# Entry into the up-projections of a two-layer trunk: the closing norms and the first unit as a written table of named pieces

## The chip, the cores and the metric

The kernel runs on one core of one Trainium2 chip, in float32. The metric is the device time of one execution in microseconds (us), the median of several runs. Engines: PE is the matrix engine (TensorE, PEld its weight loads), DVE is VectorE, ACT is ScalarE, POOL is GpSimd, SP issues transfers.

## What is computed

Two layers on a sequence of 1024 tokens with 1024 features. Layer 0 mixes tokens by differential attention, layer 1 by multi-head latent attention (MLA). Each is followed by a gated MLP with a causal convolution of width 3 behind its up-projection.

```python
D_MODEL = 1024; SEQ = 1024; DEPTH = 2; FFN_HIDDEN = 2816
def rms_norm(x, g):
    xf = x.astype(jnp.float32)
    y = xf * lax.rsqrt(jnp.mean(xf * xf, axis=-1, keepdims=True) + NORM_EPS)
    return (y * g.astype(jnp.float32)).astype(x.dtype)
def conv_ffn(h, w_up, conv_w, conv_b, w_down):
    u = h @ w_up
    c = lax.conv_general_dilated(
        u, conv_w[:, None, :].astype(u.dtype), window_strides=(1,),
        padding=[(CONV_WIDTH - 1, 0)], dimension_numbers=('NWC', 'WIO', 'NWC'),
        feature_group_count=u.shape[-1]) + conv_b
    g, val = jnp.split(c, 2, axis=-1)
    return (jax.nn.silu(g) * val) @ w_down
def reference(...):
    ...
    for i in range(DEPTH):
        h = rms_norm(x, attn_norm_g[i])
        ...
        x = x + attention(h, ...) @ w_o   # differential in layer 0, latent in layer 1
        h = rms_norm(x, ffn_norm_g[i])
        x = x + conv_ffn(h, ffn_w_up[i], ffn_conv_w[i], ffn_conv_b[i], ffn_w_down[i])
    return rms_norm(x, final_norm_g)
```

## The kernel before

**Products.** Each float32 operand is split into a high part in a reduced format (`high`, a cast on ACT) and a low part, the rest (`low`, a subtraction on DVE, or on POOL where `gp` is passed). `mm3` makes a product of three matmuls (lines 119 to 121). The up-projection is cut into 22 units. A unit is one gate block and one value block of 128 hidden features each, and is made of seven products instead of eight, by sums of blocks: the weights' side has A11, A12, A22 and the sums S1 to S4, the tokens' side B11, B21, B22 and the sums T1 to T4. B11, B21 come from token tiles 0 to 3 and B12, B22 from 4 to 7, each transposed by PE; index q numbers the four tiles of a half. `ORDER0` pairs them and gives the order of the products in unit 0.

**The end of the output projection.** `project_rest` takes the eight token tiles in pairs 0, 4, 1, 5, 2, 6, 3, 7. For each: the second half of the output projection, the residual add, mean square on ACT (`squares`), its power −1/2 on POOL (`root`, line 167), the norm on DVE (line 958), the transposes (`turn`, line 855), sums on DVE (`sub`, line 886) and splits. The last tile, 7, is normed in two halves of 512 columns (add at line 890, mean at 966, norm at 977). Layer 1 splits T2 and the first tile of B22 early (argument `early`); layer 0 does not, and splits T2.0 and T2.1 behind the last norm, with the lows on POOL (lines 979 to 981).

**Unit 0.** The generator `up` prepares weights: `sum_of` makes S1 to S4 (line 1042), `high` and `low` split them, `prepare(upto)` does so up to a number with the low on POOL. The seven products of unit 0 are issued as fourteen halves of 256 columns in the order of `FIRST`, 12 matmuls each. Behind each half come the adds that join the products into gate and value (lines 1131 to 1138), the next entry of `late` (transposes, sums and splits of the last tiles) and `prepare` up to the next entry of `ahead`. From unit 1 on a product is 512 columns wide, and its splits are made three and four products ahead.

**What sets the order.** From `project_rest` to the end of the up-projection PE and DVE run in the order in which the code issues (`outer`), POOL in the entry as well (`inner`). ACT's order in the entry is chosen by the scheduler, which also orders the attentions by itself. Transfers run on SP's queue; a weight block is fetched once its buffer is free.

Of the kernel before, what the change touches and what calls it, by code (L numbers as in the profile page):

```python
# [13 lines left out]
ALU = mybir.AluOpType  # L14
# [4 lines left out]
P = 128  # L19
# [37 lines left out]
class Trunk:  # L57
# [767 lines left out]
    def project_rest(self, W, o_d, os, X, at, x_d, g, junk, places, sums, early, begin):  # L825
# [20 lines left out]
        def normed(i, cols):  # L846
            return ends[cols.start] if i == NT - 1 else X[i][:, cols]

        def turn(i):
            names = ("B11", "B21") if i < 4 else ("B12", "B22")  # L850
            for name, cols in zip(names, (first, rest)):
                ps = banks[name, i % 4] = self.bank("u" if name == "B22" else "b")
                x = normed(i, cols)
                for k in range(4):
                    nc.tensor.transpose(ps[:, k * P : (k + 1) * P], x[:, k * P : (k + 1) * P], self.ident)
# [31 lines left out]

        def add(i, y, cols=slice(0, D)):
            x, to = X[i]
            dve.tensor_add(to[:, cols], x[:, cols], y[:, cols])  # L890

        def store(i):
            X[i] = X[i][1]
            nc.sync.dma_start(x_d[i * P : (i + 1) * P, :], X[i])

        def both(name, q, eng=dve):
            high(name, q)
            low(name, q, eng)
# [58 lines left out]
                        both("T2", q, gp)  # L957
            dve.scalar_tensor_tensor(X[before], X[before], r.pop(before), g, ALU.mult, ALU.mult)
# [7 lines left out]
        dve.tensor_scalar(s1, s1, 1.0 / D, EPS, ALU.mult, ALU.add)  # L966
        add(7, y, rest)
        s2 = self.squares(X[7][1][:, rest], junk[:, rest])
        store(7)
        start.sum("S1")  # L970
        sub("T4", 2)
        high("B11", 3)
        r7 = self.root(s2, D, s1)
        start.part(2, dve)
        for cols, place in ((first, "h12"), (rest, "h13")):
            ends[cols.start] = self.at(place, [P, 512])
            dve.scalar_tensor_tensor(ends[cols.start], X[7][:, cols], r7, g[:, cols], ALU.mult, ALU.mult)
        high("B21", 3)
        if "T2" not in early:
            both("T2", 0, gp)  # L980
            both("T2", 1, gp)
        low("B11", 3)
        low("B21", 3)

        def steps(*todo, now=lambda: None):
            def then():
                for f, *args in todo:
                    f(*args)

            return now, then  # L990

        late = [
            steps(),
            steps(),
            steps((copy, 3), (high, "B22", 3), (sub, "T1", 3), (both, "T1", 3, gp), (sub, "T3", 3), (low, "B22", 3), now=lambda: turn(7)),
            steps((sub, "T2", 3), (sub, "T4", 3)),
            steps((both, "T3", 0), (both, "T4", 0)),
            steps(*(() if "T2" in early else ((both, "T2", 2),)), (both, "T3", 1)),
            steps((both, "T2", 3), (both, "T4", 1)),
            steps((both, "T3", 2), (both, "T3", 3)),  # L1000
            steps((both, "T4", 2)),
            steps((both, "T4", 3)),
        ]
# [5 lines left out]
    ORDER0 = [("A11", "B11"), ("A12", "B21"), ("S1", "T1"), ("S4", "B22"), ("S2", "T2"), ("S3", "T3"), ("A22", "T4")]  # L1009


    FIRST = [(j, slice(256 * half, 256 * half + 256)) for j, half in (
        (0, 0), (1, 0), (2, 0), (0, 1), (1, 1), (3, 0), (2, 1), (3, 1), (4, 0), (4, 1), (5, 0), (5, 1), (6, 0), (6, 1))]

    def up(self, layer, pl, g_d, follow):

# [11 lines left out]
        def fetch(f):  # L1028
            if f < NF:
                raws[f] = [self.fetch(a["ffn_up"][layer, half * NF + f], D) for half in range(2)]  # L1030

        def sum_of(f, name):
            (gate, val) = raws[f]
            if (f, name) not in made:
                x, y, op = {
                    "S1": lambda: (val[:, first], val[:, rest], ALU.add),
                    "S2": lambda: (sum_of(f, "S1"), gate[:, first], ALU.subtract),
                    "S3": lambda: (gate[:, first], val[:, first], ALU.subtract),
                    "S4": lambda: (gate[:, rest], sum_of(f, "S2"), ALU.subtract),
                }[name]()  # L1040
                made[f, name] = sums([P, 512])
                nc.vector.tensor_tensor(made[f, name], x, y, op)  # L1042
            return made[f, name]

        def high(upto):

            while done.hi <= upto:
                n = done.hi
                done.hi += 1
                f = n // 7  # L1050
                if f >= NF:
                    continue
                name = order(n)[0]
                gate, val = raws[f]
# [21 lines left out]
            high(n)  # L1076
            low(n, eng or nc.gpsimd)

        T, late, region, inner = yield SimpleNamespace(part=part, sum=lambda name: sum_of(0, name))

        def products(n, out, cols, onto=False):
            w, t = W[n], T[order(n)[1]]
            for k in range(4):
                wh, wl = (w[:, part, k * P : (k + 1) * P] for part in range(2))
                rh, rl = (t[part][:, k, cols] for part in range(2))
                self.mm3(out, wh, wl, rh, rl, k == 0 and not onto, k == 3, onto)
# [22 lines left out]

            return SimpleNamespace(base=base, tap=tap, silu=silu, gated=gated, store=store)  # L1110

        sum_of(0, "S4")
        high(3)

        ahead = [3, 3, 3, 3, 3, 5, 6, 7, 8, 8, 8, 9, 9, 10]
        one, two = self.big(), self.big()
        bank = dict(A11=one[:, rest], S1=one[:, first], S3=one[:, rest], A22=two[:, first], S4=two[:, rest], A12=two[:, first])
        outs = {}
        for j, cols in self.FIRST:
            name = order(j)[0]  # L1120
            out = outs.get(j, bank.get(name))
            if out is None:
                out = outs[j] = self.bank("u")
            products(j, out[:, cols], cols)
            now, then = late.pop(0) if late else (lambda: None, lambda: None)
            if cols.stop == 512:
                if name == "A11":
                    u = gate, val = [self.at(place, [P, S]) for place in pl.u[:2]]
                    nc.scalar.copy(val[:, first], out)
                elif name == "S2":  # L1130
                    add(gate[:, rest], out, val[:, first])
                elif name == "S3":
                    add(val[:, rest], out, gate[:, rest])
                    add(gate[:, rest], bank["S1"], gate[:, rest])
                elif name == "A12":
                    add(gate[:, first], out, val[:, first])  # L1136
                elif name == "A22":
                    add(val[:, first], out, val[:, rest])
                    add(val[:, rest], bank["S1"], val[:, rest])
                if j == 6:  # L1140
                    add(gate[:, rest], bank["S4"], gate[:, rest])
            now()
            if j == 1:
                low(3, nc.gpsimd)
            then()
            upto = ahead.pop(0)
            if upto == 7 and 1 not in raws:
                fetch(1)
            prepare(upto)


        inner.close()
# [1156 lines left out]
```

## Time and profile before

| what | us |
|---|---|
| three runs | 2411.99, 2414.26, 2412.88 |
| median | 2412.88 |
| the profiled execution | 2414.68 |
| its span | 2412.9 |
| its mean granted clock of PE | 0.995 |

All durations below come from the profiled execution; its own time is 1.8 above its span and 1.8 above the median of the runs. A row of a timeline gives the start from the span's begin, the length, engine, line, operation, output and inputs, shapes and count, and in brackets the idle time before it with what ended it. A row of a group ends in busy time, mean length in ns, and idle time before. Lengths of pipelined matmuls overlap: start to start counts. Buffers are named by place and number (u3, h12, s9; b, u, S and big ones are PSUM), so names tell the kind of tile and not its content.

### The profile page before, as it was taken

How to read it: one execution, taken by the hardware profiler on the slowest of the kernel's cores; microseconds unless marked ns; L12 is line 12 of the kernel's file. 1: busy time of each engine (PE TensorE's matmuls, PEld its weight loads, DVE VectorE, ACT ScalarE, POOL GpSimd, SP SyncE). 2: the span in 40 equal slices, each digit the busy share in tenths (PEclk: the TensorE clock that was granted, in tenths of full speed). 3: DMA queues.
4: the chain of work that ended last, by engine and by line, in shares of the span. 5: the costliest groups of instructions: out<-in, count | busy, mean ns of one | idle time of the engine just before them, and what ended most of it. 6: DMA issues, size and time to landing. Idle time of an engine off the chain costs nothing.

```text
span 2412.9 us, 32605 instructions
## 1 busy us (share of the span) xinstructions
PE 2353.4 (98%) x11936; PEld 2000.5 (83%) x11936; DVE 1953.6 (81%) x3175; ACT 1290.7 (53%) x2366; POOL 621.2 (26%) x489
## 2 busy tenths in 40 slices
PE   7999999999999999999999999999999999999998
PEld 7888888887888888788898789988888888887886
DVE  6888888758888888899864788886588888888997
ACT  5677767744444444444445777775354444443443
POOL 4555555324000000000132666664330000000001
PEclk9999999999999999999999999999999999999999
DMA  4111111333222222643222111123322222227502
GB/s 154 40 36 36 36 48 53 110 109 106 79 79 88 88 79 79 231 166 98 81 90 64 60 40 40 40 93 107 114 71 88 87 79 79 87 83 275 175 1 79
DMA packets 95792, 213.91 MB, mean 89 GB/s; under 512 B 8720, under 2 KB 33936, under 8 KB 95632
## 3 DMA queue, kind: packets, MB, share of 16 engines
q1 hardware_dynamic: 86448, 184.04, 23.0%
q10 hardware_dynamic: 9184, 27.79, 3.1%
q8 instruction: 94, 1.54, 0.3%
q14 instruction: 66, 0.54, 0.1%
HBM read 159.37 MB, written 52.43 MB: 88 GB/s over the span
## 4 chain that ended last, share of the span: by engine, by line
PE 85%; DVE 6%; ACT 3%; DMA 3%; POOL 1%; issue 1%; SPq 0%; POOLq 0%; DVEq 0%; ACTq 0%
PE S L119 13%; PE S L121 13%; PE S L120 13%; PE b L119 8%; PE b L120 8%; PE b L121 8%; PE u L119 4%; PE u L121 4%; PE u L120 4%; PE b L252 2%; PE u L2015 1%; DVE s L130 1%; PE u L2014 1%; PE S L1859 1%; PE S L1858 1%
## 5 line engine op out<-in xcount | busy, mean ns | idle before, releaser
L167 POOL TENSOR_TENSOR st<-st,mhalf 128x1 f32<-128x1 f32 x56 | 36.6, 655 | 1314.6 <-DVE st L164 1305.3
L119 PE MATMUL S<-s,u 128*128 128x512 f32 (+1 forms) x800 | 304.0, 380 | 6.8 <-DVE u L1136 3.7
L121 PE MATMUL S<-s,u 128*128 128x512 f32 (+1 forms) x800 | 303.0, 379 | 0.1
L120 PE MATMUL S<-s,u 128*128 128x512 f32 (+1 forms) x800 | 302.7, 378 | 0.0
L127 ACT CAST u<-h 128x512 fp32r<-128x512 f32 (+2 forms) x242 | 145.8, 619 | 279.9 <-DVE h L1042 278.9
L119 PE MATMUL b<-s,u 128*128 128x512 f32 x588 | 231.0, 393 | 1.8 <-DVE u L130 1.2
L120 PE MATMUL b<-s,u 128*128 128x512 f32 x588 | 229.3, 390 | 0.0
L121 PE MATMUL b<-s,u 128*128 128x512 f32 x588 | 229.2, 390 | 0.0
L1099 DVE SCALAR_TENSOR_TENSOR u<-u,conv,u 128x1023 f32<-128x1023 f32 (+1 forms) x176 | 225.7, 1283 | 1.4 <-ACT u L1095 1.4
L149 POOL TENSOR_TENSOR u<-u,st 128x512 f32<-128x512 f32 (+7 forms) x160 | 172.0, 1084 | 168.5 <-DVE st L2000 105.0
L127 ACT CAST s<-u 128x512 fp32r<-128x512 f32 (+3 forms) x230 | 144.7, 665 | 103.1 <-PE u L121 37.2
L119 PEld LDWEIGHTS S<-s,u 128*128 128x128 f32 x800 | 152.1, 190 | 35.6 <-ACT s L127 4.0
L130 DVE TENSOR_TENSOR u<-b,u 128x512 fp32r<-128x512 f32 (+1 forms) x256 | 158.7, 631 | 20.8 <-ACT u L127 18.2
L121 PEld LDWEIGHTS S<-s,u 128*128 128x128 f32 x800 | 152.0, 190 | 28.1 <-DVE u L130 0.5
L120 PEld LDWEIGHTS S<-s,u 128*128 128x128 f32 x800 | 152.1, 190 | 27.3
L127 ACT CAST u<-b 128x512 fp32r<-128x512 f32 (+1 forms) x256 | 134.9, 546 | 72.0 <-PE b L1905 40.5
L119 PE MATMUL u<-s,s 128*128 128x512 f32 (+1 forms) x408 | 163.4, 401 | 1.9 <-DVE s L130 0.9
L130 DVE TENSOR_TENSOR s<-u,s 128x512 fp32r<-128x512 f32 (+2 forms) x210 | 151.1, 754 | 9.7 <-ACT s L127 9.4
L121 PE MATMUL u<-s,s 128*128 128x512 f32 (+1 forms) x408 | 158.8, 389 | 0.0
L120 PE MATMUL u<-s,s 128*128 128x512 f32 (+1 forms) x408 | 158.6, 389 | 0.0
L1102 ACT ACTIVATE u<-u 128x1024 f32<-128x1024 f32 x44 | 46.7, 1062 | 187.7 <-DVE u L1099 187.6
L130 DVE TENSOR_TENSOR u<-h,u 128x512 fp32r<-128x512 f32 x164 | 112.8, 688 | 32.5 <-ACT u L127 31.5
(280 smaller groups left out, 6544.1 us busy)
## 6 DMA issues: line engine op xcount, KB each, us to landing
u<-in_ffn_up SPq DMA_DIRECT2D x88, 512.0 KB, 3.9
g_d<-u ACTq DMA_DIRECT2D x44, 512.0 KB, 2.6
u<-in_ffn_down SPq DMA_DIRECT2D x66, 256.0 KB, 5.0
u<-g_d SPq DMA_DIRECT2D x62, 256.0 KB, 4.4
s<-in_da_wqkv SPq DMA_DIRECT2D x23, 512.0 KB, 3.6
x_d<-u SPq DMA_DIRECT2D x16, 512.0 KB, 3.0
s<-x_d SPq DMA_DIRECT2D x8, 1024.0 KB, 10.8
u<-o_d SPq DMA_DIRECT2D x24, 256.0 KB, 3.0
```

What stands on the lines that cost most here:

```text
L119: mm(out, lh, rl, start=first, stop=False, skip_group_check=onto)
L120: mm(out, lh, rh, start=False, stop=False, skip_group_check=onto)
L121: mm(out, ll, rh, start=False, stop=last, skip_group_check=onto)
L127: self.nc.scalar.copy(out, src)
L130: (eng or self.nc.vector).tensor_sub(out, src, hi.bitcast(F32))
L149: self.nc.gpsimd.tensor_mul(x, x, s.to_broadcast(list(x.shape)))
L167: nc.gpsimd.tensor_tensor(r, s, self.mhalf, ALU.pow)
L252: self.nc.tensor.transpose(ps[:, j * P : (j + 1) * P], probs[t][:, k : k + P], self.ident)
L1099: nc.vector.scalar_tensor_tensor(t[half][:, back:], u[half][:, : S - back], w, t[half][:, back:], ALU.mult, ALU.add)
L1102: nc.scalar.activation(t[0], t[0], AF.Silu)
L1858: nc.tensor.matmul(sc[c][:, b : b + m], ql[c][:, qs], kt[:, c, :m], start=True, stop=False)
L1859: nc.tensor.matmul(sc[c][:, b : b + m], qh[:, c, qs], kt[:, c, :m], start=False, stop=True)
```

## The change

The closing norm of tile 7, the last transposes, sums and splits, the split of the weights of products 1 to 10, the fourteen halves of unit 0 and the adds behind them become named pieces: `x`, `ya`, `yb` are transposes (tile 3; tile 7, first and second half), `xa`, `xb` the two halves of the residual add, `xs`, `xq` their squares, `xt` the mean, `xr` the root, `ea`, `eb` the norm halves; `T1.3s`, `T1.3h`, `T1.3l`, `T1.3g` a sum, its high, its low on DVE, its low on POOL, for tile 3 of T1; `w4h`, `w4l`, `w4g` the same for the weights of product 4; `sS1`, `tS1` sums of unit 0 and of unit 1; `p3a`, `p3b` the halves of product 3; `c0` to `e6` the adds; `f1` the fetch of unit 1's weights. A table `CLOSE` lists them once for each layer, in the order in which they are issued. ACT is put under the written order in the entry as well.

```diff
-        def turn(i):
+        def turn(i, which=3):
...
-            for name, cols in zip(names, (first, rest)):
+            for name, cols in list(zip(names, (first, rest)))[which == 2 : which]:
...
-        y = ys[NT - 1]
-        turn(3)
-        X[7] = X[7], at(7, X[7])
-        add(7, y, first)
-        s1 = self.squares(X[7][1][:, first], junk[:, first])
-        start.part(1)
-        dve.tensor_scalar(s1, s1, 1.0 / D, EPS, ALU.mult, ALU.add)
-        add(7, y, rest)
...
-        if "T2" not in early:
-            both("T2", 0, gp)
-            both("T2", 1, gp)
...
-        return T, late, outer, inner
+        tokens = {}
+
+        def put(name, f, *args):
+            tokens[name] = lambda: f(*args)
+
+        put("x", turn, 3)
+        put("xa", end_add, first)
...
+        put("ya", turn, 7, 1)
+        put("yb", turn, 7, 2)
+        put("B12.3c", copy, 3)
+        for name in ("B11", "B21", "B22", "T1", "T2", "T3", "T4"):
+            for q in range(4):
+                put(f"{name}.{q}s", sub, name, q)
+                put(f"{name}.{q}h", high, name, q)
+                put(f"{name}.{q}l", low, name, q)
+                put(f"{name}.{q}g", low, name, q, gp)
+        return T, tokens, outer, inner
...
-    FIRST = [(j, slice(256 * half, 256 * half + 256)) for j, half in (
-        (0, 0), (1, 0), (2, 0), (0, 1), (1, 1), (3, 0), (2, 1), (3, 1), (4, 0), (4, 1), (5, 0), (5, 1), (6, 0), (6, 1))]
+    CLOSE = (
+        (
+            "x w1h xa w1g xs xb sS1 T4.2s B21.3h xt xq w2h T2.1h T4.0h xr T2.0h B21.3l w2l B11.3h ea eb p1a sS2 p2a sS4 w3h yb",
...
+        (
...
+            "T2.3g T1.3l p1b w6h w5l T4.3s T3.2h w6l T4.1g f1 T4.2h T4.3h p4a p5a T4.3l T3.3h p2b w7h T3.3g p4b c1 T3.2g tS1 tS3",
...
-        for j, cols in self.FIRST:
...
-                elif name == "A12":
-                    add(gate[:, first], out, val[:, first])
...
-            prepare(upto)
+            c1=lambda: add(gate_of(first), outs[1], val_of(first)),
...
+        inner.enter_context(self.tc.manual_schedule(engines={mybir.EngineType.Activation}))
+        for name in " ".join(self.CLOSE[layer]).split():
+            tokens[name]()
+        gate, val = u
```

The orders below stand at three places. First VectorE in layer 0, from the norm of tile 6 on (L958 above it): L890 the residual add of tile 7, L1042 (L1056 after) the sum S1 of the weights, L886 a sum of tokens, L130 a low, L977 (L981) the norm halves h12, h13. Before:

```order
L890 TENSOR_TENSOR u7_1061_5743<-s11_957_5148,S_1048_5672 128x512
L966 TENSOR_SCALAR st1_1062_5745<-st1_1062_5745 128x1
L890 TENSOR_TENSOR u7_1061_5743<-s11_957_5148,S_1048_5672 128x512
L1042 TENSOR_TENSOR h9_1065_5755<-u15_1052_5709 128x512
L886 TENSOR_TENSOR u6_1045_5659<-b_1042_5626,u2_1035_5600 128x512
L166 SCALAR_TENSOR_TENSOR st1_1064_5752<-st1_1064_5752,st1_1062_5745 128x1
L130 TENSOR_TENSOR u11_1067_5762<-h9_1065_5755,u11_1067_5762 128x512
L977 SCALAR_TENSOR_TENSOR h12_1068_5765<-u7_1061_5743,st1_1066_5759,u9_975_5296 128x512
L977 SCALAR_TENSOR_TENSOR h13_1069_5767<-u7_1061_5743,st1_1066_5759,u9_975_5296 128x512
L130 TENSOR_TENSOR s1_1000_5427<-b_1059_5733,s0_999_5426 128x4x128
L130 TENSOR_TENSOR s3_1003_5432<-b_1060_5738,s2_1002_5431 128x4x128
```

and in the changed kernel:

```order
L890 TENSOR_TENSOR u7_1064_5749<-s11_957_5148,S_1048_5672 128x512 x2
L1056 TENSOR_TENSOR h9_1066_5755<-u15_1052_5709 128x512
L886 TENSOR_TENSOR u6_1045_5659<-b_1042_5626,u2_1035_5600 128x512
L974 TENSOR_SCALAR st1_1065_5752<-st1_1065_5752 128x1
L166 SCALAR_TENSOR_TENSOR st1_1067_5760<-st1_1067_5760,st1_1065_5752 128x1
L130 TENSOR_TENSOR s3_1003_5432<-b_1062_5742,s2_1002_5431 128x4x128
L130 TENSOR_TENSOR u11_1068_5763<-h9_1066_5755,u11_1068_5763 128x512
L981 SCALAR_TENSOR_TENSOR h12_1074_5778<-u7_1064_5749,st1_1073_5771,u9_975_5296 128x512
L981 SCALAR_TENSOR_TENSOR h13_1075_5780<-u7_1064_5749,st1_1073_5771,u9_975_5296 128x512
L1056 TENSOR_TENSOR h10_1076_5794<-h9_1066_5755,u14_1051_5707 128x512
```

The two halves of the add stand together, the mean (L966, now L974) behind them; the low of B21.3 (s3) has moved ahead of the norm halves and that of B11.3 (s1) further back. Second GpSimd in layer 0, around the root of tile 7 (L167); s11 are lows of T2, u10 and s13 those of later weights and tokens. Before:

```order
L130 TENSOR_TENSOR u13_1063_5747<-u14_1051_5707,u13_1063_5747 128x512
L167 TENSOR_TENSOR st1_1066_5759<-st1_1064_5752,mhalf_119 128x1
L130 TENSOR_TENSOR s11_1071_5771<-u0_989_5373,s10_1070_5770 128x4x128
L130 TENSOR_TENSOR s11_1071_5771<-u1_1011_5481,s10_1070_5770 128x4x128
L130 TENSOR_TENSOR u10_1074_5782<-h11_1073_5780,u10_1074_5782 128x512
L130 TENSOR_TENSOR s13_1017_5495<-h7_1080_5836,s12_1016_5494 128x4x128
```

and in the changed kernel:

```order
L130 TENSOR_TENSOR u13_1063_5747<-u14_1051_5707,u13_1063_5747 128x512
L167 TENSOR_TENSOR st1_1073_5771<-st1_1067_5760,mhalf_119 128x1
L130 TENSOR_TENSOR u10_1078_5810<-h11_1077_5808,u10_1078_5810 128x512
L130 TENSOR_TENSOR s11_1070_5766<-u0_989_5373,s10_1069_5765 128x4x128
L130 TENSOR_TENSOR s5_1084_5845<-u4_998_5423,s4_1083_5844 128x4x128
```

The two lows of T2 no longer follow the root directly: one has gone behind the low of S4's weights, the other to VectorE. Third PE at the start of the MLA attention, which the table does not list; S are score matmuls, L252 transposes, L2014 and L2015 (L2033 and L2034 after) products of weights with values, b_2126 a projection. Before:

```order
L121 MATMUL S_2138_12634<-s12_1963_11882,s5_2015_12099 128x256
L252 MATMUL b_2114_12542<-ident_113,u8_2097_12468 128x128 x3
L119 MATMUL b_2126_12588<-s2_1819_10968,u2_2058_12294 128x512
L120 MATMUL b_2126_12588<-s2_1819_10968,u2_2058_12294 128x512
L121 MATMUL b_2126_12588<-s2_1819_10968,u3_2059_12295 128x512
```

and in the changed kernel:

```order
L121 MATMUL S_2138_12637<-s12_1963_11885,s5_2015_12102 128x256
L119 MATMUL S_2146_12679<-s8_1964_11886,s9_2048_12250 128x384
L120 MATMUL S_2146_12679<-s8_1964_11886,s9_2048_12250 128x384
L121 MATMUL S_2146_12679<-s8_1964_11886,s9_2048_12250 128x384
L252 MATMUL b_2114_12545<-ident_113,u8_2097_12471 128x128 x3
L2033 MATMUL u_2108_12517<-u0_2101_12491,s4_2010_12089 128x256
```

The score matmuls S_2146 stand ahead of the transposes, and the products u_2108 ahead of the projection b_2126, behind which both stood before. The count of matmuls is the same in both kernels; POOL has 484 instructions instead of 489 and DVE five more.

More of the change, by code (lines that the diff above doesn't have):

```diff
@@ L972, in project_rest @@
[L972 to L978, printed above, removed]
-        if "T2" not in early:
-            both("T2", 0, gp)
-            both("T2", 1, gp)
[L982 to L1003, printed above, removed]
@@ L1004, in project_rest, with end_add, end_squares, end_mean @@
-        return T, late, outer, inner
+        last, st = ys[NT - 1], SimpleNamespace()
+        def end_add(cols):
+            if cols == first:
+                X[7] = X[7], at(7, X[7])
+            add(7, last, cols)
+        def end_squares(name, cols):
+            to = X[7][1] if cols == first else X[7][1]
+            setattr(st, name, self.squares(to[:, cols], junk[:, cols]))
+            if cols == rest:
+                store(7)
+        def end_mean():
+            dve.tensor_scalar(st.s1, st.s1, 1.0 / D, EPS, ALU.mult, ALU.add)
@@ new lines, in end_root, with end_norm @@
+        def end_root():
+            st.r = self.root(st.s2, D, st.s1)
+        def end_norm(cols):
+            ends[cols.start] = self.at("h12" if cols == first else "h13", [P, 512])
+            dve.scalar_tensor_tensor(ends[cols.start], X[7][:, cols], st.r, g[:, cols], ALU.mult, ALU.mult)
+        tokens = {}
[3 more added lines that the diff above has]
+        put("xa", end_add, first)
+        put("xb", end_add, rest)
+        put("xs", end_squares, "s1", first)
@@ L1077, in part @@
             low(n, eng or nc.gpsimd)
-        T, late, region, inner = yield SimpleNamespace(part=part, sum=lambda name: sum_of(0, name))
+        T, tokens, region, inner = yield SimpleNamespace(part=part)
         def products(n, out, cols, onto=False):
@@ L1118, in up, with begin, product @@
         outs = {}
-        for j, cols in self.FIRST:
-            name = order(j)[0]
-            out = outs.get(j, bank.get(name))
+        u = []
+        gate_of = lambda cols: u[0][:, cols]
+        val_of = lambda cols: u[1][:, cols]
+        def begin():
+            u.extend(self.at(place, [P, S]) for place in pl.u[:2])
+            nc.scalar.copy(val_of(first), outs[0])
+        def product(j, cols):
+            out = outs.get(j, bank.get(order(j)[0]))
             if out is None:
                 out = outs[j] = self.bank("u")
+            outs[j] = out
@@ L1124, in up @@
             products(j, out[:, cols], cols)
[L1125 to L1134, printed above, removed]
-                elif name == "A12":
[L1136 to L1148, printed above, removed]
-            prepare(upto)
+        for j in range(7):
+            tokens[f"p{j}a"] = lambda j=j: product(j, slice(0, 256))
+            tokens[f"p{j}b"] = lambda j=j: product(j, slice(256, 512))
+        for n in range(1, 11):
+            tokens[f"w{n}h"] = lambda n=n: high(n)
+            tokens[f"w{n}l"] = lambda n=n: low(n)
+            tokens[f"w{n}g"] = lambda n=n: low(n, nc.gpsimd)
@@ new lines, in up @@
+        for name in ("S1", "S2", "S3", "S4"):
+            tokens["s" + name] = lambda name=name: sum_of(0, name)
+            tokens["t" + name] = lambda name=name: sum_of(1, name)
+        tokens.update(
+            f1=lambda: fetch(1),
+            c0=begin,
+            c1=lambda: add(gate_of(first), outs[1], val_of(first)),
+            c4=lambda: add(gate_of(rest), outs[4], val_of(first)),
+            c5=lambda: add(val_of(rest), outs[5], gate_of(rest)),
+            d5=lambda: add(gate_of(rest), bank["S1"], gate_of(rest)),
+            c6=lambda: add(val_of(first), outs[6], val_of(rest)),
+            d6=lambda: add(val_of(rest), bank["S1"], val_of(rest)),
+            e6=lambda: add(gate_of(rest), bank["S4"], gate_of(rest)),
+        )
```

15 lines of the change are left out of this document (8 added, 7 removed), and 6 rows, old and new, of the table CLOSE.

## The prediction

> **What bounds the kernel now.** I read the head of the page, then the chain that ended last, then a table of windows over the three stretches in which the order changes.
>
> ```profile
> span 2412.9 us, 32605 instructions
> PE 2353.4 (98%) x11936; PEld 2000.5 (83%) x11936; DVE 1953.6 (81%) x3175; ACT 1290.7 (53%) x2366; POOL 621.2 (26%) x489
> PE 85%; DVE 6%; ACT 3%; DMA 3%; POOL 1%; issue 1%; SPq 0%; POOLq 0%; DVEq 0%; ACTq 0%
> ```
>
> TensorE is busy 98% of the span and the number of its matmuls stays, so all that the change can win are stretches in which TensorE stands or crawls. The windows below are: the entry of layer 0, from the transposes of token tile 3 to the first matmul of unit 1; the equally long stretch behind it; the same two for layer 1; and the start of the MLA attention. Columns: start and end, length, busy time and count of PE, PEld, DVE, ACT, POOL, granted clock, DMA share, GB/s.
>
> ```profile
> 571.89:602.51 30.62, 25.49 (x184) 23.77 (x185) 28.56 (x36) 11.50 (x23) 16.22 (x11) 0.94 0.26 87
> 602.51:633.13 30.62, 30.62 (x137) 25.36 (x136) 25.31 (x33) 15.06 (x21) 2.56 (x2) 1.00 0.22 70
> 1755.06:1783.24 28.18, 24.45 (x186) 23.54 (x186) 25.47 (x35) 12.67 (x26) 15.15 (x11) 0.94 0.23 76
> 1783.24:1811.42 28.18, 28.18 (x127) 23.34 (x126) 23.40 (x30) 13.90 (x19) 2.55 (x2) 1.00 0.17 57
> 1347.00:1432.00 85.00, 84.05 (x536) 75.57 (x536) 67.51 (x162) 61.85 (x137) 56.35 (x45) 0.99 0.13 37
> ```
>
> Behind the entries PE is busy throughout; in them it loses time, and its clock is 0.94. In layer 0 VectorE is busy 28.56 of 30.62 us: it is the engine that paces that entry. An entry is 168 matmuls of 256 columns and 16 transposes. What they cost end to end is read from starts that follow each other without a wait (start, length, engine, line):
>
> ```profile
> 590.23 0.28 PE L119 MATMUL S<-s,u 128*128 128x256 f32 x1
> 590.35 0.28 PE L120 MATMUL S<-s,u 128*128 128x256 f32 x1
> 571.89 1.07 PE L855 MATMUL b<-ident,u 128*128 128x128 f32 x8 [0.82 <-DVE u L958]
> 572.71 0.36 PE L119 MATMUL S<-s,u 128*128 128x256 f32 x1
> ```
>
> A matmul takes 0.12 us from start to start, so 168 take 20.2; eight transposes take 0.82, so 16 take 1.6. That stream is 21.8 us. Layer 0 lost 30.6 − 21.8 = 8.8 us in the entry, layer 1 28.2 − 21.8 = 6.4. Where it went, first by what PE waited for (us in total, times, longest; layer 0, then layer 1):
>
> ```profile
> PE S L119 <- DVE s L130: 1.7, 2, 1.1
> PE u L855 <- DVE h L977: 1.1, 1, 1.1
> PE S L119 <- DVE u L1136: 1.1, 1, 1.1
> PE b L855 <- DVE h L977: 0.8, 1, 0.8
> PE S L119 <- DVE u L890: 0.2, 1, 0.2
> PE S L119 <- POOL s L130: 0.2, 1, 0.2
> ```
>
> ```profile
> PE S L119 <- DVE u L1136: 2.6, 1, 2.6
> PE S L119 <- DVE u L890: 1.0, 1, 1.0
> ```
>
> and then by the clock (window of 3.41 us, PE busy and count, granted clock, DMA share, GB/s):
>
> ```profile
> 577.79:581.20 3.41, 1.54 (x12) 1.00 0.00 0
> 581.20:584.61 3.41, 3.41 (x17) 0.50 0.02 5
> 1765.62:1769.03 3.41, 0.81 (x7) 1.00 0.01 2
> 1769.03:1772.44 3.41, 3.41 (x19) 0.50 0.00 0
> 1757.36:1760.77 3.41, 2.33 (x18) 1.00 0.38 154
> 2200.30:2203.71 3.41, 1.86 (x9) 1.00 1.05 386
> ```
>
> In both entries a window in which PE was busy 1.54 or 0.81 us is followed by one at half clock, which does 1.7 us of work in 3.41 and so costs 1.7. Windows with 1.86 and 2.33 busy were not followed by a drop. That is 1.7 of the loss in each entry; the rest is waits: 8.8 − 1.7 = 7.1 in layer 0 (5.1 recorded, plus some 0.16 for each of seven waits, since a record lasts 0.28 where the next starts after 0.12, plus short waits and changes of shape), 4.7 in layer 1 (3.6 recorded).
>
> The Trainium skill, TensorE: Matmul & The Clock Gate, Part 1, has the free-running window of 3413 ns and lets the clock fall only after an idle one. The rows above agree on the length, but the clock fell after windows that were 45% and 24% busy; by the page no stop here (at most 2.6 us) would have cost clock, and the sum below would be 3.4 smaller, 2410.4. The measured rows decide.
>
> **The change, part by part.**
>
> *Layer 0, the norm of the last tile.* The transposes of the last tile wait 0.8 and 1.1 for the two norm halves:
>
> ```profile
> 573.79 0.16 DVE L966 TENSOR_SCALAR st<-st 128x1 f32<-128x1 f32 x1 [1.45 <-ACT u L157]
> 573.87 0.68 DVE L890 TENSOR_TENSOR u<-s,S 128x512 f32<-128x512 f32 x1
> 575.89 1.05 POOL L167 TENSOR_TENSOR st<-st,mhalf 128x1 f32<-128x1 f32 x1 [3.02 <-DVE st L166]
> 576.92 2.96 POOL L130 TENSOR_TENSOR s<-u,s 128x512 fp32r<-128x512 f32 x2
> 576.98 3.45 DVE L977 SCALAR_TENSOR_TENSOR h<-u,st,u 128x512 f32<-128x512 f32 x2 [0.44 <-POOL st L167]
> 580.57 0.63 PE L855 MATMUL u<-ident,h 128*128 128x128 f32 x4 [1.11 <-DVE h L977]
> 1760.92 1.41 DVE L977 SCALAR_TENSOR_TENSOR h<-u,st,u 128x512 f32<-128x512 f32 x2 [0.44 <-POOL st L167]
> ```
>
> Two things are changed. The second residual add stood behind the small mean, which waited 1.45 us for ScalarE; now both adds go back to back, so the second starts at about 572.2 instead of 573.87, and the sums, squares and the power with it (1.4 us earlier: power about 574.4, norm halves from 575.5). And the two lows of T2 that GpSimd ran beside the norms are gone from there: beside them the halves took 3.45, in layer 1, where GpSimd has nothing beside, 1.41. So the halves end at about 576.9 instead of 580.43, 3.5 earlier. The transposes follow at 577.1 and 577.5, with 0.15 of wait, where before the second four stood at 580.57.
>
> What is late next is the split of the S1 weights, whose high is a ScalarE cast of 0.62:
>
> ```profile
> L127 ACT CAST u<-h 128x512 fp32r<-128x512 f32 (+2 forms) x242 | 145.8, 619 | 279.9 <-DVE h L1042 278.9
> ```
>
> I walk the new order with the rows' durations, each instruction starting when its engine and its sources are free. The sum S1 runs on VectorE behind the two adds, 572.8 to 573.5; its cast stands behind the square of the second half and is done at 574.8, which holds PE 0.6; its low on VectorE, until 575.6, holds PE another 0.6. After 577.1 no piece waits; the margins run from 0.5 (at 582.5) to 4 us. Waits left: 0.6 + 0.6 + 0.15 = 1.35, against 5.5 for the same walk of the old order (0.3, 0.6, 0.5, 1.4, 0.15, 1.1, 0.2, 0.2, 1.1). Gain in waits 4.2. In the 3.41 us of 574 to 577.4 PE would be busy over 2 us, above the 1.86 that kept the clock, so the half-clock window goes as well: 1.7. **Layer 0: −5.9**; unit 1 starts near 596.5.
>
> *VectorE as cover.* Its busy 28.56 us falls with the entry only if it has less to do, since unit 1 needs its splits. It does:
>
> ```profile
> L130 DVE TENSOR_TENSOR s<-u,s 128x512 fp32r<-128x512 f32 x9 | 10.3, 1191 | 0.0
> L130 DVE TENSOR_TENSOR s<-b,s 128x512 fp32r<-128x512 f32 x2 | 1.3, 676 | 0.0
> 586.90 1.74 POOL L130 TENSOR_TENSOR s<-h,s 128x512 fp32r<-128x512 f32 x1
> 585.67 1.27 POOL L130 TENSOR_TENSOR u<-h,u 128x512 fp32r<-128x512 f32 x1 [5.79 <-ACT u L127]
> ```
>
> A low whose source is in PSUM takes 0.68 on VectorE; the nine with both sources in SBUF average 1.19, because some ran beside GpSimd's, which grow from 1.27 to 1.74 at the same time. Nine times 0.51 is 4.6 us, and the norms above lost another 2.0 to it. In the new table layer 0 has five GpSimd subtractions fewer and three VectorE ones more in all. Three at 0.68 cost 2.0 and at least five collisions of about 0.5 to 1.1 go: 2.5 to 5.5. VectorE comes out 0.5 to 3.5 ahead, before the norms' 2.0. That cover is what the 0.5 margin hangs on; were it gone, each further collision would cost up to 1.1.
>
> *Layer 1.* The norms collide with nothing there, so less is to be had. The 2.6 us wait ends on the add of L1136 (gate of A12), which in program order stood before S4's first half and on VectorE behind a row of other operations. As `c1` it now stands behind p4b, and S4's first half (`p3a`) well ahead of it, so that this piece no longer waits for it. Walked waits: 4.2 before (1.1, 0.6, 2.5), 2.4 after (1.7 at 1757.3, where the low of the second weights stands behind the adds and one low, and 0.7 at 1767.7). Gain 1.8 in waits and 1.7 in clock is 3.5; my walk of the old order is 0.9 us later than the trace in this stretch, so I take between: **layer 1: −3.0**, bounds −1.2 (the clock falls anyway) to −3.5. One fetch is exposed: the sums of unit 1 need weights whose buffer GpSimd frees at 1772.4;
>
> ```profile
> u<-in_ffn_up SPq DMA_DIRECT2D x88, 512.0 KB, 3.9
> ```
>
> with 3.9 us to landing VectorE stands about 3 us at 1773.4 to 1776.6, and the last low that unit 0 needs keeps 0.3 us of margin. SP's two swapped issues are this fetch and its partner.
>
> *MLA start.* Its instructions are not in the table, but its order has come out differently: score matmuls and transposes have been drawn ahead of products. Before, PE lost little there:
>
> ```profile
> PE b L119 <- DVE u L130: 0.9, 2, 0.5
> ```
>
> The walk gives 1.5 us of waits before and 3.9 after; a part is made up before the stretch ends. **+1.2**, bounds +0.9 and +2.3. ScalarE's order in the entries is fixed now as well; with 11.5 and 12.7 us busy of about 30 it costs nothing beyond the 0.6 above.
>
> *Sum.* −5.9 − 3.0 + 1.2 = −7.7. The profiled execution took 2414.68, 1.8 above the runs' median of 2412.88, about one half-clock window. If it is one of the two in the entries that the median run lacks, the median falls by only 6.0, to 2406.9; if it lies elsewhere, it falls by 7.7 to 2405.2; from the profiled time the sum gives 2407.0. I take 2406.8.
>
> **The rivals.**
>
> *The clock still drops in layer 1.* The 1.7 us wait from 1757.3 lies in the window 1757.36 to 1760.77, busy 2.33 with a recorded wait of 1.0 before. With 1.5 recorded it would be busy about 1.8, between 1.54, which cost the clock, and 1.86, which did not. For: a low that is 0.2 us later than walked is enough; against: 1.8 is much nearer to 1.86. +1.7 on the sum: 2408.5. 24%.
>
> *The MLA start costs more.* Three new waits there end on ScalarE's and VectorE's exponential chain, whose durations in the new neighbourhood no row shows. At the whole 3.9 us without anything made up, and a little of clock, it is +4 instead of +1.2: 2409.6. 7%.
>
> *Slower: collisions of VectorE and GpSimd make VectorE the bound of both entries.* GpSimd still has some ten subtractions in each, and they fall where the table puts them, against VectorE lows of 1.19 mean and norm halves of up to 1.72. Each collision more than walked costs up to 1.1, once VectorE's surplus is used up (2.5 in layer 0 from above, 3 in layer 1 from its stand at the fetch). The gain is gone from (7.7 + 5.5) / 1.1 = 12 of them on. Were all ten in each entry to hit anew, 11 us each, layer 0 would be 11 − 2.5 − 5.9 = 2.6 longer, layer 1 11 − 3 − 3 = 5.0, and the MLA start 1.2: 8.8 over the runs' median, about 2422. For it: nine lows already lose 4.6 us, and who starts first is a matter of tenths. Against: the old order, with five more of GpSimd's in layer 0, still lost no more than 8.8 there. 5%. The Trainium skill, SBUF — State Buffer, section SBUF: two separate sides, calls that pair of ports an exclusive lock, held for the whole instruction by whoever starts first; by it the loser of each pair would stand for the other's full 1.3 us, 13 instead of 11 in each entry.
>
> *More is won.* Layer 1 gives its full 3.5, the MLA start takes 0.9, and all of it shows against the median: 2412.9 − 5.9 − 3.5 + 0.9 = 2404.4. For it: both are bounds from above; against: the walk of layer 1 was late by 0.9. 9%.
>
> **How the numbers follow.** My forecast with small spread has 55%. About 0.2% (4.8 us) is what a measurement of this kernel can tell from no change: faster means under 2408.05, slower over 2417.7. Forecast and large gain are 64%, and of the clock rival, whose 2408.5 lies just beyond that bound, a third lands below it: 0.72 faster. The rest of it and the MLA rival are 0.23; slower 0.05. The range holds the clock rival and most of the MLA one and reaches down to the larger gain: 2404.0 to 2410.5.
>
> **What would show it.** In the new trace: norm halves of about 0.75 us each ending near 577 in layer 0; no window at clock 0.50 in 571 to 600 or in the 30 us of layer 1's entry; unit 1 of layer 0 starting near 596.5, and of layer 1 near 1783.2 − 7.7 = 1775.5. Wrong would be: VectorE lows of 1.7 on PE's waits (collisions), a PE wait over 2.5 us in layer 1's entry, or PE idle growing by over 3 us in 1341 to 1426.

## The result, and the profile after

| | before | changed |
|---|---|---|
| median of eight runs, us | 2412.41 | 2405.53 |
| lowest to highest | 2411.36 to 2414.26 | 2402.48 to 2407.88 |
| profiled execution, us | 2414.68 | 2402.48 |

The ratio is 0.997 (0.9962 to 0.9979): 6.9 us less, where 2406.8 was forecast (6.1 under the median shown then). The profiled execution of the changed kernel is the fastest of its eight runs, so its trace shows a larger difference, 12.2 us. The windows below answer to those of before: layer 0's entry, layer 1's entry, the MLA start (there from the same pair of matmuls in both kernels; for before the row is shown first).

```profile
1341.18:1432.10 90.92, 87.94 (x551) 78.45 (x551) 71.72 (x173) 66.63 (x145) 62.17 (x48) 0.98 0.14 42
```

```profile
570.36:595.01 24.65, 23.09 (x186) 22.18 (x185) 24.23 (x36) 14.25 (x29) 11.39 (x9) 1.00 0.31 108
1748.12:1773.61 25.49, 22.92 (x186) 22.13 (x186) 21.93 (x34) 12.95 (x26) 11.85 (x10) 1.00 0.26 84
1333.29:1425.22 91.93, 87.05 (x551) 77.12 (x552) 72.25 (x175) 66.53 (x145) 62.16 (x48) 1.00 0.14 41
```

Layer 0's entry is 30.62 − 24.65 = 6.0 shorter, layer 1's 28.18 − 25.49 = 2.7, both at full clock now. The MLA start is 1.0 longer although its clock had been 0.98 and is 1.00. VectorE in layer 0 fell from 28.56 to 24.23 us busy: it still fills the entry. What PE waits for in the changed kernel's two entries (first layer 0, then layer 1), and over the whole MLA start, before and changed:

```profile
PE S L121 <- DVE u L130: 0.8, 1, 0.8
PE S L121 <- POOL u L130: 0.7, 1, 0.7
```

```profile
PE S L119 <- DVE s L130: 1.9, 2, 1.7
PE u L121 <- DVE u L130: 0.6, 1, 0.6
```

```profile
PE S L119 <- ACT u L1994: 2.8, 3, 1.4
PE b L119 <- DVE u L130: 0.9, 2, 0.5
```

```profile
PE S L119 <- ACT u L2013: 4.3, 5, 1.4
PE u L2033 <- DVE u L130: 0.7, 1, 0.7
PE b L252 <- DVE S L2011: 0.5, 1, 0.5
PE b L252 <- DVE u L130: 0.2, 1, 0.2
```

Seven waits in layer 0, 5.1 us, have become two of 1.5; in layer 1 3.6 have become 2.5; at the MLA start 3.7 have become 5.7. The next rows are the norm of tile 3 and the norm halves of tile 7, both on VectorE, and the root on GpSimd. The section on the change calls the norm at L958 that of tile 6; it is that of tile 3, which stands ahead of tile 7 in the pairs and whose transposes wait for it.

```profile
568.18 1.76 DVE L958 SCALAR_TENSOR_TENSOR u<-u,st,u 128x1024 f32<-128x1024 f32 x1
574.92 1.41 DVE L981 SCALAR_TENSOR_TENSOR h<-u,st,u 128x512 f32<-128x512 f32 x2
573.88 0.55 POOL L167 TENSOR_TENSOR st<-st,mhalf 128x1 f32<-128x1 f32 x1 [1.56 <-DVE st L166]
```

The halves take 1.41 instead of 3.45 and end at 576.3 instead of 580.4. The rest of the 12.2 lies outside: 1.5 ahead of layer 0's entry, 2.6 behind layer 1's, where this execution lacks a half-clock window that the other had at 2216, and 0.4 between layer 0's entry and the MLA start.

### The profile page after: what moved, and what is told of

It is laid out like the page before. It is cut to its first block, busy times and chain, and to the rows that moved or that the text cites. A ratio compares the mean times of both kernels' runs of the same rounds, so it can differ in the third digit from the quotient of the medians.

```text
span 2400.7 us, 32598 instructions
## 1 busy us (share of the span) xinstructions
PE 2345.5 (98%) x11936; PEld 1993.4 (83%) x11936; DVE 1947.9 (81%) x3180; ACT 1290.0 (54%) x2366; POOL 612.4 (26%) x484
## 4 chain that ended last, share of the span: by engine, by line
PE 85%; DVE 6%; DMA 3%; ACT 3%; POOL 2%; issue 2%; SPq 0%; POOLq 0%; DVEq 0%; ACTq 0%
PE S L119 13%; PE S L121 13%; PE S L120 13%; PE b L119 8%; PE b L120 8%; PE b L121 8%; PE u L119 4%; PE u L121 4%; PE u L120 4%; PE b L252 2%; PE u L2034 1%; PE u L2033 1%; PE S L1878 1%; PE S L1877 1%; DMA u<-g_d 1%
## 5 line engine op out<-in xcount | busy, mean ns | idle before, releaser
L167 POOL TENSOR_TENSOR st<-st,mhalf 128x1 f32<-128x1 f32 x56 | 36.1, 645 | 1312.7 <-DVE st L164 1304.9
L130 DVE TENSOR_TENSOR u<-b,u 128x512 fp32r<-128x512 f32 (+1 forms) x256 | 159.0, 632 | 21.6 <-ACT u L127 19.0
L130 DVE TENSOR_TENSOR s<-u,s 128x512 fp32r<-128x512 f32 (+2 forms) x204 | 139.1, 714 | 9.2 <-ACT s L127 8.9
L130 DVE TENSOR_TENSOR u<-h,u 128x512 fp32r<-128x512 f32 x171 | 117.4, 687 | 32.6 <-ACT u L127 31.5
```

The costliest lines, as they stand in the source:

```text
L130: (eng or self.nc.vector).tensor_sub(out, src, hi.bitcast(F32))
L167: nc.gpsimd.tensor_tensor(r, s, self.mhalf, ALU.pow)
```

## The experiments

Times are medians; the ratio to the kernel before, measured beside each on the same chip, has its 95% interval. The kernel before took 2412.41 beside the changed kernel, 2412.74 beside e1 to e4, 2412.61 beside e5 to e7 and 2413.18 beside e8 to e10. Because one half-clock window more or less moves a run by up to 1.7 us, the trace's stretches are given beside each time: an entry runs from the transposes of tile 3 to the first matmul of unit 1, the MLA start between the same two matmuls as above; in brackets half of the time that it spent at half clock, which is the most that this can have cost. It costs less where PE would have waited: the MLA start in its old order takes 90.12 with none (e8) and 91.63 with 3.4 (e10).

| kernel | time, us | ratio | layer 0's entry | MLA start | layer 1's entry |
|---|---|---|---|---|---|
| before | 2412.41 | | 30.62 (1.7) | 90.92 (1.7) | 28.18 (1.7) |
| changed | 2405.53 | 0.9962 to 0.9979 | 24.65 | 91.93 | 25.49 |
| e1 layer 1 only | 2409.46 | 0.9980 to 0.9997 | 29.61 (1.7) | 91.07 (1.7) | 25.40 |
| e2 ScalarE free | 2408.22 | 0.9970 to 0.9988 | 25.61 | 91.00 (1.7) | 28.33 |
| e3 lows beside norm | 2406.60 | 0.9967 to 0.9986 | 26.58 | 92.19 (1.7) | 25.66 |
| e4 mean between adds | 2403.86 | 0.9953 to 0.9978 | 24.97 | 91.11 (1.7) | 25.72 |
| e5 one low earlier | 2404.03 | 0.9946 to 0.9971 | 25.45 | 91.03 (3.0) | 25.71 |
| e6 gate add ahead | 2407.32 | 0.9965 to 0.9986 | 25.47 | 91.04 (3.2) | 29.25 (1.7) |
| e7 old order, ScalarE fixed | 2419.99 | 1.0018 to 1.0037 | 32.51 (1.7) | 91.50 (3.1) | 31.67 (1.4) |
| e8 layer 0 only | 2406.29 | 0.9960 to 0.9982 | 25.44 | 90.12 | 28.16 (1.7) |
| e9 changed, again | 2404.40 | 0.9953 to 0.9978 | 24.62 | 92.82 (3.4) | 27.42 |
| e10 as e5, again | 2404.47 | 0.9948 to 0.9975 | 25.44 | 91.63 (3.4) | 25.59 |

**e1: layer 1's table alone.** Layer 0 runs the old code.

```diff
-        up = k.up(0, pl, g_d[0], follow)
-        operands = k.project_rest(
+        up = k.up_old(0, pl, g_d[0], follow)
+        operands = k.project_rest_old(
```

> Layer 0 keeps the old order and layer 1 alone has its table; the MLA start then stands as before. Theory (the two entries gain separately, 6 us in layer 0 and 3 in layer 1): layer 1's entry about 3 us shorter, layer 0's unchanged with its two late norm halves of 1.7 us each and its half-clock window, time 3 under before, about 2409.5. Rival (layer 1 owes its gain to the window of half clock alone): the waits of layer 1's entry sum to as much as before, and its time is within 1.7 of before, 2410.7 to 2412.4.

3.3 us faster; layer 1's entry is 25.40 as in the changed kernel, layer 0's 29.61 with its late norm halves and its half-clock window, and the MLA start stands as before. The rival, that only a window of half clock had been gained, would have left layer 1's waits as they were: they fell from 3.6 to 2.4.

**e8: layer 0's table alone**, with the one low of e5 moved so that the MLA start keeps its old order; layer 1 runs the old code.

```diff
-        up = k.up(1, pl, g_d[1], follow)
-        operands = k.project_rest(
+        up = k.up_old(1, pl, g_d[1], follow)
+        operands = k.project_rest_old(
```

> Layer 0 has its table (with the one low moved, so that the MLA start stands as before) and layer 1 keeps the old order: only layer 0's entry differs from the kernel before. Theory (the parts add up): layer 0's entry 6 us shorter, layer 1's as before with its 2.5 us wait on the gate's add; 2406.0 to 2407.0, and with the 3.3 measured for layer 1 alone it makes the 8.6 of both. Rival (the two entries share a part of the gain, such as a window of half clock that only moves on): under 4.5 gained, over 2408.

6.9 us faster; layer 0's entry 25.44, layer 1's 28.16 with the old wait and its half clock:

```profile
PE S L119 <- DVE u L1132: 2.6, 1, 2.6
...
PE S L119 <- DVE u L890: 1.0, 1, 1.0
```

6.9 and 3.3 make 10.2, and both with the old MLA start gave 8.6 (e5) and 8.7 (e10). In the traces the parts add up better: 5.2 and 2.8 of entry are 8.0, where both entries together gave 7.6 (e5) and 7.8 (e10). The difference in the times is within the intervals of about 2.5 us each.

**e2: ScalarE's order free.** The tables stay.

```diff
-        inner.enter_context(self.tc.manual_schedule(engines={mybir.EngineType.Activation}))
```

> The tables stay, but ScalarE's order in the entries is left to the scheduler as before; this also gives the MLA start its old order back. Theory of the prediction (ScalarE's fixed order is worth nothing, the new order of the MLA start costs 2.3): entries as in the changed kernel, 2.3 gained at the MLA start, about 2403.2. Rival (the fixed order of ScalarE is a part of the gain, because a cast that a low and a piece of PE wait for is otherwise behind squares and casts that nobody waits for yet): layer 0's entry 2 us longer than in the changed kernel, with PE waits of 1.2 and 0.8 and two of 0.6; layer 1's up to 4 longer, with waits of 2.2, 1.7 and 1.8; with the 2.3 gained about 2409.5.

The rival holds, at somewhat less than the size it was given. In layer 0 PE waits on ScalarE's cast (first row), and layer 1 loses its whole gain, 28.33 at full clock, with the waits of the other rows:

```profile
PE S L119 <- ACT u L127: 1.0, 1, 1.0
```

```profile
PE S L119 <- DVE s L130: 2.1, 1, 2.1
PE b L855 <- DVE u L886: 1.5, 1, 1.5
...
PE S L121 <- DVE u L130: 0.6, 1, 0.6
```

ScalarE in layer 1 shows why. Casts keep it busy from 1750.52 to the square of tile 7's first half, which starts at 1753.61, although the residual add that it needs began at 1751.89 and took 0.7; in the changed kernel (last row) ScalarE is free and the square starts as soon as that add is done:

```profile
1750.52 2.71 ACT L127 CAST s<-u 128x512 fp32r<-128x512 f32 x5 [0.20 <-PE S L121]
1753.61 0.63 ACT L157 ACTIVATE u<-u 128x512 f32<-128x512 f32 x1
```

```profile
1749.10 0.63 ACT L157 ACTIVATE u<-u 128x512 f32<-128x512 f32 x1 [1.52 <-DVE u L890]
```

The MLA start has its old order. The two entries are 25.61 + 28.33 − 24.65 − 25.49 = 3.8 longer, and the stretch ahead of layer 0's entry is 1.0 longer (last section); 1.2 is given back at the MLA start, and the time is 2.7 longer. So 3.8 us of the entries' gain hang on ScalarE following the table, the engine that is busy 53% of the span in the kernel before. The rest does not: with ScalarE free the tables are still 4.5 us faster than the kernel before, and layer 0's entry keeps 5.0 of its 6.0.

**e7: that fixing alone.** The old code, with ScalarE held to its issue order.

```diff
+        inner.enter_context(self.tc.manual_schedule(engines={mybir.EngineType.Activation}))
         ahead = [3, 3, 3, 3, 3, 5, 6, 7, 8, 8, 8, 9, 9, 10]
```

> The kernel before with one part of the change alone: ScalarE held to the order in which the old code issues, in both entries. Theory (fixing ScalarE pays only with the table, since in the old code casts stand behind casts that nobody needs yet): layer 0's entry 2.5 longer than before, with PE waits of 2.5 and 3.0, layer 1's 2.1 longer with waits of 2.4 and 3.2; about 2417. Rival (the fixed order is by itself worth the 2 and 4 us that freeing it cost): about 2406 to 2408.

2419.99 against 2412.61 for the kernel before on the same chip, 7.4 slower. The direction was expected, the size was not: layer 0's entry is 1.9 longer, layer 1's 3.5 and the MLA start 0.6. The profiled executions are 4.3 apart, so the rest of the 7.4 is not placed by a trace. The longest waits in layer 0:

```profile
PE S L119 <- DVE s L130: 3.2, 2, 2.3
PE u L855 <- DVE h L977: 1.1, 1, 1.1
PE S L119 <- DVE u L1137: 1.0, 1, 1.0
```

So the fixing is worth something only with the table, in which casts stand in the order of need; the table is worth 4.5 us without the fixing (e2), 5.0 in layer 0's entry and nothing in layer 1's.

**e3: the two lows of T2 back beside the norm.**

```diff
-            "... xr T2.0h B21.3l ... yb", "T2.1l w3g ... p0b T2.0g ...",
+            "... xr T2.0h T2.0g T2.1g B21.3l ... yb", "w3g ... p0b ...",
```

> One part of the table undone in layer 0: the lows of T2.0 and T2.1 go back onto GpSimd right behind the root, beside the two norm halves. Theory (VectorE and GpSimd exclude each other there): the norm halves take about 3.4 us together instead of 1.4, VectorE is 1.5 to 2 us late behind them, and PE waits about 1.5 for the low of B22.3 (the product S4's second half); entry 1.5 longer, time about 2407.0, the MLA start as in the changed kernel. Rival (the two adds side by side made the gain, the lows are hidden by the margins): norm halves long, but no new PE wait over 0.3, time 2405.5.

VectorE first, then GpSimd, then what PE waits for:

```profile
575.40 2.44 DVE L981 SCALAR_TENSOR_TENSOR h<-u,st,u 128x512 f32<-128x512 f32 x2
577.76 1.75 DVE L1056 TENSOR_TENSOR h<-h,u 128x512 f32<-128x512 f32 x1
575.79 3.18 POOL L130 TENSOR_TENSOR s<-u,s 128x512 fp32r<-128x512 f32 x2 [0.88 <-ACT s L127]
```

```profile
PE u L855 <- DVE h L981: 1.0, 1, 1.0
PE S L121 <- DVE u L130: 0.8, 1, 0.8
PE S L121 <- POOL u L130: 0.7, 1, 0.7
PE S L119 <- DVE s L130: 0.6, 1, 0.6
```

The two GpSimd lows stretch one norm half and the sum behind it, 1.0 us each (2.44 for two against 1.41, 1.75 for one against 0.68). The entry is 1.9 longer, where 1.5 was expected, and the new waits sit on the norm half (1.0) and a low (0.6), where a wait of 1.5 on the low alone was expected.

**e4: the mean between the two adds again.**

```diff
-            "x w1h xa w1g xs xb sS1 T4.2s B21.3h xt xq ...",
+            "x w1h xa w1g xs xt xb sS1 T4.2s B21.3h xq ...",
```

> One part of the table undone in layer 0: the small mean stands between the two halves of the residual add again, where VectorE waits for ScalarE's square. This also gives the MLA start its old order back, with ScalarE's order still fixed. Theory: VectorE waits about 1 us at the mean, PE's waits on the split of the S1 weights grow by 0.4 and 0.3, layer 0's entry is 0.75 longer, and 2.3 is gained at the MLA start: about 2404.0. Rival (the new order of the MLA start costs nothing): about 2406.3.

```profile
573.00 0.15 DVE L974 TENSOR_SCALAR st<-st 128x1 f32<-128x1 f32 x1 [0.85 <-ACT u L157]
```

VectorE waits 0.85 us for the square again and the entry is 0.3 longer; 0.75 was expected. This swap of two pieces gives the MLA start its old order: 91.11, where the changed order at the same half clock (e3) has 92.19.

**e6: the gate's add ahead of S4** (on e5's table).

```diff
-            "... T3.0g w4h T4.0g sS3 p3a T4.1h ... T1.3l p1b w6h ... w7h T3.3g p4b c1 T3.2g ...",
+            "... T3.0g w4h T4.0g sS3 T4.1h ... T1.3l p1b c1 p3a w6h ... w7h T3.3g p4b T3.2g ...",
```

> As the previous kernel, and in layer 1's table the add c1 (gate of A12) goes directly behind p1b and the first half of S4 (p3a) behind it, as both stood before the change. Theory (that add, behind a row of lows on VectorE, held p3a for 2.6 us before): PE waits 2.6 us on that add again and 1.0 on a low ahead of it, layer 1's entry is 3.0 longer than in the previous kernel, 4.7 if a window falls to half clock: 2406.5 to 2408. Rival (another wait takes its place there in any order): entry within 0.7 of the previous kernel.

```profile
PE S L119 <- DVE s L130: 2.6, 2, 1.6
PE S L119 <- DVE u L1157: 2.5, 1, 2.5
```

The 2.5 us wait is back, and a half-clock window with it: the entry is 29.25 − 25.71 = 3.5 longer than in e5, the time 3.3.

**e5, e9, e10: what the reordered MLA start costs.** One low is moved in layer 0, the MLA start has its old order.

```diff
-            "... B12.3c B22.3h T1.3s p1b ... p0a B22.3l T1.3l p0b ...",
+            "... B12.3c B22.3h B22.3l T1.3s p1b ... p0a T1.3l p0b ...",
```

> The changed kernel with one entry of layer 0's table moved: the low of B22.3 stands ahead of T1.3s instead of behind p0a. By the walk that costs layer 0's entry 0.1; ScalarE stays fixed, layer 1's table is the same, and the MLA start has its old order again. Theory (the reordered MLA start costs 1.3 to 2.3): entries as in the changed kernel to 0.3, waits at the MLA start back to about 0.9 on VectorE's low, about 2403.5. Rival (the reorder costs nothing, the difference in the earlier traces was the half-clock window): 2405.5.

> The changed kernel once more, beside the next one on one chip, to settle what the reordered MLA start costs. Theory: 1.2 to 2.3 slower than the next one, about 2405.5; waits at the MLA start on ScalarE, VectorE and on a product of weights and values. Rival: equal within 0.5.

> The kernel with the low of B22.3 moved once more. Theory: about 2404.0, that is 1.2 to 2.3 under the changed kernel. Rival: equal within 0.5. Beside that: if the store of tile 6's tokens again lands after 2.6 us, with the instruction load behind 570 instead of within the store, the connection seen in nine traces holds in an eleventh.

The first time it was 1.5 us faster than the changed kernel, side by side it was equal (2404.47 and 2404.40), so the times do not settle it. The stretches do, with one trace for most of the values: at the same half clock the new order is longer by 91.93 − 90.12 = 1.8 (none), 92.19 − 91.03 = 1.2 (1.7, e3 against the mean of before, e1, e2, e4) and 92.82 − 91.63 = 1.2 (3.4). The times hid it because the moved low costs layer 0's entry 0.8 instead of the 0.1 that I walked. None of these versions beats the changed kernel by more than its interval; e4, with 24.97 and the old MLA start, has the shortest sum of stretches.

## Why the prediction was right, step by step

**Layer 0, −5.9: measured −6.0**, by the mechanism named: halves of 0.7 us without GpSimd beside them, five stops gone, no half-clock window. The parts that were undone one at a time cost 1.9 (e3), 0.3 (e4) and 1.0 (e2, ScalarE's order, which the forecast did not price); with the window's 1.7 that is 4.9, and which part took the window away was not tried. The waits left sum to 1.8 (recorded 1.5, and 0.3 for the overlap of records) against 1.35, but they are other ones: not the cast of the S1 weights, but the GpSimd low of A12's (0.7), then VectorE's low of S1's (0.8). That fits the transposes of tile 3, which came 1.0 us earlier than in before for a reason that the prediction does not have (last section): in e2, where they came late again, the wait on the GpSimd low is absent and the cast is waited for (1.0). One count was wrong: up to the MLA start GpSimd has three instructions fewer (269 instead of 272), not five, since the other two are layer 1's. The cover of VectorE held all the same.

**Layer 1, −3.0: measured −2.7** in the changed kernel's trace, −2.5 to −2.8 in e1, e3, e4, e5 and e10, and −0.8 in e9. The wait on the gate's add was the cause (e6). The 0.3 us of margin at the fetch of unit 1's weights was real: in e9 that fetch landed late, VectorE stood 5.18 us instead of 3.26 for it, and PE waited 2.1 for the low behind. The rows are of the changed kernel, then of e9:

```profile
1770.13 0.69 DVE L1056 TENSOR_TENSOR h<-u 128x512 f32<-128x512 f32 x1 [3.26 <-DMA u<-in_ffn_up]
```

```profile
1774.25 0.69 DVE L1056 TENSOR_TENSOR h<-u 128x512 f32<-128x512 f32 x1 [5.18 <-DMA u<-in_ffn_up]
```

**MLA start, +1.2: measured +1.2 to +1.8** at equal clock. Without half clock the recorded waits are 4.3 in the old order (e8) and 5.7 in the new, 1.4 more, where the walk had 2.4 more. It is a side effect, not of the table, but of what the scheduler makes of it: swapping two pieces in layer 0 (e4), or leaving ScalarE free there (e2), takes it back.

**ScalarE: this step failed.** The prediction gave its fixed order no price because ScalarE is idle half of the time. It was worth 1.0 in layer 0's entry and 2.8 in layer 1's (e2), and by itself it costs 7.4 (e7). The sum came out all the same because the walk followed the new ScalarE order (it puts the cast of S1 behind the square of the second half); the text did not name it as a term.

**The clock.** No entry with the table had a half-clock window, except e6's in layer 1, which was provoked. The rival that layer 1 would drop anyway did not occur, but not by a clear margin: its window was busy 1.70 us:

```profile
1750.08:1753.49 3.41, 1.70 (x15) 1.00 0.38 154
```

By the count in the last section 12 of 28 such windows were followed by half clock. In e5, e6, e9 and e10 the same window was busy 1.72 to 1.86, and none of the five fell; nothing here shows why, so that this rival stayed away may be luck.

The collision rival (slower) is refuted as well: VectorE's busy time in layer 0 fell by 4.3 us, and no wait of PE there is longer than 0.8.

**The number.** That the three stretches of the profiled execution make −6.0 − 2.7 + 1.0 = −7.7, exactly the forecast's sum, is in part chance, since the MLA start had half clock in one trace and none in the other. The 1.0 us ahead of layer 0's entry is in the measured gain and not in the sum. And the step from 7.7 to 6.1 rests on a half-clock window that the median run was supposed to lack, which no run tested: the changed kernel fell by 6.9 the first time and by 8.8 in e9 (2404.40 against 2413.18).

## What to carry to other kernels

In this kernel a written order paid where engines hand work to each other every half microsecond, and it paid in full only when every engine in the chain followed it: leaving an idle-looking ScalarE free lost 3.8 us of the two entries, and fixing ScalarE on an order not written for it lost 7.4. Look first for what runs beside the engine that paces the stretch and slows it (two norm halves took 3.45 us beside GpSimd's lows, 1.41 without), then for what an early wait holds up behind it. And look at the order of the whole program after a local change: 1.2 to 1.8 of the gain went in a stage 740 us later that nobody had touched.

## What the runs showed of the hardware beyond that

**An 8 KB instruction load went with a late store.** Tile 3 (tile 6 in the expectation of e10) is normed in place once its store has landed. In before, e1, e2 and e7 that store took 3.2 us, in the other eight traces 2.6. The four, and only they, have an instruction load within it (before, then changed; queue, packets, MB, share, and the store's time to landing):

```profile
q14 instruction: 1, 0.01, 0.6%
...
x_d<-u SPq DMA_DIRECT2D x1, 512.0 KB, 3.2
```

```profile
x_d<-u SPq DMA_DIRECT2D x1, 512.0 KB, 2.6
```

In before the norm started together with a GpSimd subtraction, and took 2.38 us:

```profile
569.37 2.38 DVE L958 SCALAR_TENSOR_TENSOR u<-u,st,u 128x1024 f32<-128x1024 f32 x1 [0.65 <-DMA x_d<-u]
```

In the changed kernel it took 1.76 and stood 1.2 earlier, 0.5 of which the trace led by already; PE's wait of 0.8 for it went. From the transposes of tile 6 to those of tile 3 the four kernels take 7.3 us and the other eight 6.3 to 6.4, so 1.0 of the gain lies here, in every kernel that has layer 0's table and ScalarE fixed. In the kernels with 2.6 the load comes behind 570. That the load delays the store is what the twelve traces fit, not what an experiment shows, and whose load it is stays open: ScalarE idles there for 4.05 us in the changed kernel, but for 4.71 in e7, where the load falls into the store.

**When the clock falls.** Laid over all twelve traces behind the first 20 us, at the phase of the windows of 3.41 us: of the windows at full clock in which PE was busy 1.6 us or less (nine at the end, in which it had stopped, left out), all 30 were followed by half clock; of those with 1.61 to 1.95, 12 of 28; of those with more, none of 8246. The busiest of the twelve (in e5), and one of the thirty (in the changed kernel):

```profile
1331.25:1334.66 3.41, 1.93 (x11) 1.00 0.45 181
```

```profile
453.02:456.43 3.41, 1.48 (x9) 1.00 0.45 167
```

The Trainium skill, TensorE: Matmul & The Clock Gate, Part 1, speaks of an idle window; here a window busy by up to 1.6 of its 3.41 us is enough. The phase of the windows differs from run to run, so the same stops fall into one window or two: leaving out its first 20 us and its last windows, the changed kernel had one half-clock window in its first trace, with a span of 2400.7 us, and four in e9's, with 2404.9. That is one reason why executions of one kernel differ by some us, and why stretches of a trace settled here what medians could not.
